# A two-layer bidirectional encoder trunk on one core: the convolution gate as 512-column products, and five small moves around it

## The chip, the cores and the metric

The kernel runs on one core of a Trainium2 chip. The metric is the time of one execution on the device in microseconds (us); lower is better. The engines are TensorE (PE; its weight loads are listed as PEld), VectorE (DVE), ScalarE (ACT), GpSimd (POOL) and SyncE (SP, which only issues DMAs here). Each engine works through its own list of instructions in order and waits on semaphores.

## The reference

Sequence 256, width 2048, two layers. Cut to what matters:

```python
h = x
for i in range(DEPTH):                       # DEPTH = 2
    hn = _rmsnorm(h, norm_g[i])
    u = hn @ w_in[i]
    a_val, a_glu, a_z, q, k, v, b_z = jnp.split(u, offs, axis=-1)
    ya = _conformer_conv(a_val, a_glu, ...)  # GLU, depthwise conv (31 taps), LayerNorm, SiLU
    ya = ya * jax.nn.silu(a_z)               # the convolution gate
    yb = _window_attention(q, k, v, bias_band, sink[i]) * jax.nn.silu(b_z)
    h = h + jnp.concatenate([ya, yb], axis=-1) @ w_out[i]
    e = _rmsnorm(p[i] @ w_pe[i], pe_g[i])
    h = h + e * jax.nn.sigmoid(h @ w_pg[i])  # the gate of the per-layer embedding
return _rmsnorm(h, final_g)
```

## The kernel before, in words

Everything is held with channels on the 128 partitions and the 256 positions along the free axis, so a tile of a product is 128 x 256. To keep float32 accuracy, activations and weights are split into a high part (rounded) and a low part (the rest): ACT casts the high part (L163 for weights), DVE subtracts (L166). A product is then high x high + high x low + low x high. mm3 has two forms. The narrow one adds three 256-column products into one half of a PSUM bank (L402 to L404). The wide one (wide, L399 and L400) streams both parts of the activations through the high weights at once, 512 columns, into the two halves of a bank, and adds the low weights' 256-column product to the second half; the two halves must then be added, which merge does with a copy on ACT (L410) and an add on DVE (L411).

Weights come in halves of 128 x 1024, eight k tiles of 128 columns each, in the order of weight_halves(), which is the order in which PE uses them. step takes one half and ends in a pump, which lets work written as generators go on: the convolution (conv, DVE), attention, the embedding's norm, and lnorm, the layer norm behind the convolution. get asks for the split of the weights four halves ahead.

A layer runs in this order: e (p times w_pe, L498), the RMS norm of h, the value and GLU products (ag), k, v, then four pairs of attention gate (zb) and q, then four pairs of the convolution gate (za, L707 for its SiLU). The second half of the last pair is preceded by finish, which lets convolution and attention end. Then yb, the attention's result, is split (L750 on ACT, L751 on DVE), the mean of the convolution is taken by PE (L716), and the output projection goes over the yb half of its weights for all 16 tiles and then over the ya half (wide form, L776 to L778 make h and its two parts, h1). Last comes the gate of the embedding (g, wide form) with w_pg.

An inverse root mean square needs a sum over partitions: rstd_col gets it by products with a column of ones (L349), raises it to -0.5 on POOL (L356), and DVE spreads it into a diagonal (L361); rstd_row multiplies that by ones (L367) to have it in every partition. rh is the norm of h, re that of e, rv that of the convolution, rf the final one.

At the start nothing is in flight: x comes in four loads, weights and p beside them, PE multiplies zeros (warm), and ACT squares x (L385, L388, L506) while it copies e's products out of PSUM (L522); DVE adds the squares (L389) and folds them (L376).

Of the kernel before, what the change touches and what calls it, by code (L numbers as in the profile page):

```python
# [54 lines left out]
AW = (0,0,0,0)  # L55
NWARM = 4
QQ = ((4, 5), (2, 4))
# [21 lines left out]
def weight_halves():  # L79
# [28 lines left out]
    for j in range(NB_FIRST, KT):  # L108
        out.append(("w_out", tile_cols(j), 8, 8))
        out.append(("w_out", tile_cols(j), 0, 8))  # L110
    for j in range(KT):
        std("w_pg", tile_cols(j))
# [13 lines left out]
def trunk_kernel(ctx: ExitStack, tc: tile.TileContext, xT, pT, wst, par, gain, relb, sinkp, onehot, out):  # L126
# [151 lines left out]
    load_half(0, 1)  # L278
    load_x(4, nc.scalar)
    load_x(0)  # L280
    load_half(1, 0, nc.scalar)
# [61 lines left out]

    def rstd_col(parts, dim, name, between=None, idles=0):

# [10 lines left out]
        nc.gpsimd.tensor_tensor(col, v, mhalf, ALU.pow)  # L356
        if between:
            between()
        dg = wk.tile([P, 2, P], F32, name=name + "dg", tag="rdg", bufs=1)
        for b in range(2):  # L360
            nc.vector.tensor_scalar(dg[:, b, :], ident, col[:, b:b + 1], None, ALU.mult)  # L361
        return dg

    def rstd_row(dg, name, tag="rb", copy=True):

        bb = bank(name + "b")
        nc.tensor.matmul(bb[:, 0, :], ones, dg.rearrange("p a b -> p (a b)"), start=True, stop=True)  # L367
        if not copy:
            return bb[:, 0, :]
        rb = wk.tile([P, S], F32, name=name + "rb", tag=tag, bufs=1)  # L370
        nc.scalar.copy(rb, bb[:, 0, :])
        return rb
# [22 lines left out]
    def mm3(o, w, x, start, stop):  # L395
# [8 lines left out]
        nc.tensor.matmul(o, w[:, 1], x[:, 0], start=False, stop=stop, skip_group_check=True)  # L404

    def merge(bs):

        t = wk.tile([P, 2, S], F32, name="hl", tag="ptt")[:, 0:len(bs), :]
        for x, b in enumerate(bs):
            nc.scalar.copy(t[:, x, :], b[:, 1, :])  # L410
            nc.vector.tensor_add(t[:, x, :], b[:, 0, :], t[:, x, :])  # L411
        return t
# [42 lines left out]
    for l in range(DEPTH):  # L455
# [21 lines left out]
        def operands(k, n):  # L477
            for k in range(k, k + 2 * n, 2):
                subs.append(operand(k))
                if len(subs) > 1:  # L480
                    subs.pop(0)()

        for q in range(4):
            n = Cursor.h
# [5 lines left out]
            for jj in range(0, 4, 2):  # L490
# [29 lines left out]
                if QQ[l][1] + (l == 0) <= j // 2 <= QQ[l][1] + 1:  # L520
                    operands(4 * (j // 2 - QQ[l][1]), 2)
                nc.scalar.copy(e[j // 8][:, j % 8:j % 8 + 2, :], b)  # L522
            pump()
# [174 lines left out]
        for t in range(0, NCT, 2):  # L698
            b = pair(hg, f"za{l}_{t}")
            if t == NCT - 2:  # L700
                finish(l)

                for k in (0, 4):
                    nc.gpsimd.dma_start(a[:, k:k + 4, :], hsrc[:, k:k + 4, :])
                yb = bigt(f"yb{l}", F32R)
                nc.scalar.copy(yb[:, 0, 0:2, :], zb[:, 0:2, :])
            nc.scalar.activation(za[:, t:t + 2, :], b, AF.Silu)  # L707

        ya = bigt(f"ya{l}", F32R)

        def lnorm(l=l, acc=acc, za=za, ya=ya, ysum=ysum, done=done):

            mb = bank("mean")
            parts = [ysum] + [acc[:, t, :] for t in done[-2:]]
            for x, a in enumerate(parts):
                nc.tensor.matmul(mb[:, 0, :], ones, a, start=(x == 0), stop=(x == len(parts) - 1))  # L716
            mu = wk.tile([P, S], F32, name="mu", tag="mu", bufs=1)
# [4 lines left out]
            for t in range(4):  # L722
                nc.vector.tensor_sub(q[t], q[t], bcast2(mu))
                square_acc(vacc, q[t], t == 0, nc.vector)
                if t % 2:
                    yield
            yield from wait(LY[0])
            dg = rstd_col(halves_of(vacc), W_CONV, f"rv{l}")
            yield from wait(LY[1])
# [94 lines left out]
        for j in range(0, KT - 2, 2):  # L824
            gate(j, merge([wide(h1, f"g{l}_{j + x}") for x in range(2)]))
            if j == 4 and not last:
                pp = wk.tile([P, 2, 2, S], F32R, name="pp", tag="qq")
                hilo(pp[:, 0], pp[:, 1], pf)
# [103 lines left out]
```

## Time and profile before

| | |
|---|---|
| runs of before | 980.79 us median of 3 (979.82 to 983.81) |
| the profiled execution's own time | 984.36 us |
| its span, first to last instruction | 982.6 us |
| mean granted clock of TensorE | 0.995 of full speed |
| busy: PE, DVE, ACT, POOL | 966.2, 796.8, 558.1, 82.2 us |

The profile is of one execution, so its rows add up to its own time, not to the median. A row of a timeline gives the start, the duration, the engine, the line of the kernel, the output and inputs, their shape and how many instructions were merged; in brackets stands how long the engine was idle before, and what ended that. Matmuls overlap, so their rate is read from start to start. A float32 product shows as two instructions.

### The profile page before, as it was taken

To read this page: it belongs to the slowest core of one execution; us is meant where nothing else is said; L and a number is where in the kernel's file an instruction comes from. 1 tells how busy PE (TensorE), PEld (TensorE's weight loads), DVE (VectorE), ACT (ScalarE), POOL (GpSimd) and SP (SyncE) were. 2 spreads that over 40 slices of the span, in tenths; PEclk is the share of its full clock that TensorE was granted. 3 is DMA by queue.
4 is the path that set the end of the run, shared out by engine and by line. 5 is a ranking of instruction groups with operands and counts; after the bars stand their busy time and mean duration, and the time that the engine had idled before them with its cause. 6 is when DMAs were issued, how large, how long until landed. Compare 5 with 4: busy or idle time off the path is not lost.

```text
span 982.6 us, 17720 instructions
## 1 busy us (share of the span) xinstructions
PE 966.2 (98%) x7196; PEld 913.1 (93%) x7196; DVE 796.8 (81%) x1383; ACT 558.1 (57%) x861; POOL 82.2 (8%) x79
## 2 busy tenths in 40 slices
PE   8999999999999999999999999999999999999995
PEld 6999999999999998888899999999999999888885
DVE  3899989987787777787689998988887877777763
ACT  4655454777774544555566444568778545445552
POOL 0022001010000000011103200000100000000111
PEclk9999999999999999999999999999999999999998
DMA  7674636555547454546546455465454555544532
GB/s 284 221 242 171 207 137 232 190 179 177 171 151 243 147 205 170 207 171 220 202 178 215 172 195 192 171 209 200 150 166 167 177 194 201 180 170 173 180 120 86
DMA packets 29005, 182.45 MB, mean 186 GB/s; under 512 B 3595, under 2 KB 4156, under 8 KB 9084
## 3 DMA queue, kind: packets, MB, share of 16 engines
q1 hardware_dynamic: 24284, 165.70, 48.3%
q0 software_dynamic: 3344, 12.88, 4.1%
q10 hardware_dynamic: 1296, 2.75, 0.8%
q8 instruction: 56, 0.92, 0.4%
q14 instruction: 25, 0.20, 0.1%
HBM read 177.09 MB, written 4.23 MB: 185 GB/s over the span
## 4 chain that ended last, share of the span: by engine, by line
PE 89%; DVE 5%; ACT 2%; issue 2%; DMA 1%; POOL 0%; SPq 0%; DVEq 0%; ACTq 0%; POOLq 0%
PE g L399 11%; PE ag L404 6%; PE ag L402 6%; PE ag L403 6%; PE g L400 5%; PE o L399 3%; PE za L402 3%; PE zb L402 3%; PE q L402 3%; PE o L402 3%; PE o L403 3%; PE o L404 3%; PE zb L403 3%; PE q L403 3%; PE za L403 3%; PE zb L404 3%
## 5 line engine op out<-in xcount | busy, mean ns | idle before, releaser
L166 DVE TENSOR_TENSOR w<-raw,w 128x1024 fp32r<-128x1024 f32 x306 | 372.8, 1227 | 102.9 <-ACT w L163 97.8
L163 ACT CAST w<-raw 128x1024 fp32r<-128x1024 f32 x308 | 314.5, 1046 | 167.3 <-PE ag L404 43.5
L572 DVE SCALAR_TENSOR_TENSOR cz<-az,pars,cz 128x241 f32<-128x241 f32 (+11 forms) x480 | 218.0, 504 | 1.0
L399 PE MATMUL g<-h,w 128*128 128x512 f32 x496 | 175.6, 399 | 2.3 <-DVE h L778 2.3
L404 PE MATMUL ag<-hg,w 128*128 128x256 f32 x512 | 145.1, 283 | 0.5 <-DVE w L166 0.5
L402 PE MATMUL ag<-hg,w 128*128 128x256 f32 x512 | 145.4, 284 | 0.0
L403 PE MATMUL ag<-hg,w 128*128 128x256 f32 x512 | 145.0, 283 | 0.0
L400 PE MATMUL g<-h,w 128*128 128x256 f32 x496 | 139.3, 281 | 0.0
L399 PEld LDWEIGHTS g<-h,w 128*128 128x128 f32 x496 | 93.2, 188 | 26.1 <-DVE h L778 2.9
L402 PEld LDWEIGHTS ag<-hg,w 128*128 128x128 f32 x512 | 98.3, 192 | 0.9 <-ACT cz L565 0.8
L404 PEld LDWEIGHTS ag<-hg,w 128*128 128x128 f32 x512 | 98.2, 192 | 0.8 <-DVE w L166 0.7
L403 PEld LDWEIGHTS ag<-hg,w 128*128 128x128 f32 x512 | 98.3, 192 | 0.1
L400 PEld LDWEIGHTS g<-h,w 128*128 128x128 f32 x496 | 93.7, 189 | 0.0
L399 PE MATMUL o<-ya,w 128*128 128x512 f32 x256 | 90.5, 399 | 0.0
L402 PE MATMUL za<-hg,w 128*128 128x256 f32 x256 | 73.7, 288 | 0.0
L402 PE MATMUL o<-yb,w 128*128 128x256 f32 x256 | 73.3, 286 | 0.0
L402 PE MATMUL q<-hg,w 128*128 128x256 f32 x256 | 73.3, 286 | 0.0
L402 PE MATMUL zb<-hg,w 128*128 128x256 f32 x256 | 73.1, 286 | 0.0
L403 PE MATMUL o<-yb,w 128*128 128x256 f32 x256 | 72.6, 283 | 0.0
L404 PE MATMUL o<-yb,w 128*128 128x256 f32 x256 | 72.4, 283 | 0.0
L403 PE MATMUL zb<-hg,w 128*128 128x256 f32 x256 | 72.4, 283 | 0.0
L403 PE MATMUL q<-hg,w 128*128 128x256 f32 x256 | 72.4, 283 | 0.0
(231 smaller groups left out, 2093.7 us busy)
## 6 DMA issues: line engine op xcount, KB each, us to landing
raw<-in_wst SPq DMA_DIRECT2D x153, 1024.0 KB, 4.9
bias<-fscr POOLq DMA_DIRECT2D x16, 384.0 KB, 3.8
raw<-in_wst SPq DMA_DIRECT2D x4, 512.0 KB, 7.9
az<-in_xT POOLq DMA_DIRECT2D x4, 512.0 KB, 6.1
hscr<-e POOLq DMA_DIRECT2D x2, 1024.0 KB, 5.0
az<-hscr POOLq DMA_DIRECT2D x4, 512.0 KB, 6.2
x<-in_xT SPq DMA_DIRECT2D x3, 512.0 KB, 8.1
out_t<-og ACTq DMA_DIRECT2D x4, 256.0 KB, 3.2
```

Of the source, the lines that this page charges most:

```text
L163: nc.scalar.copy(hi, raw)
L166: nc.vector.tensor_sub(lo, raw, hi.bitcast(F32))
L399: nc.tensor.matmul(o, w[:, 0], x, start=start, stop=False, skip_group_check=True)
L400: nc.tensor.matmul(o[:, 1], w[:, 1], x[:, 0], start=False, stop=stop, skip_group_check=True)
L402: nc.tensor.matmul(o, w[:, 0], x[:, 0], start=start, stop=False, skip_group_check=True)
L403: nc.tensor.matmul(o, w[:, 0], x[:, 1], start=False, stop=False, skip_group_check=True)
L404: nc.tensor.matmul(o, w[:, 1], x[:, 0], start=False, stop=stop, skip_group_check=True)
L572: nc.vector.scalar_tensor_tensor(acc[:, t, lo_:hi_], a[:, t, lo_ + s:hi_ + s], w(k), acc[:, t, lo_:hi_], ALU.mult, ALU.add)
```

## The change

- The convolution gate uses the wide form, one bank for each of the 16 tiles. A pair is merged (L408 and L409 in the new file) before its SiLU, for the last pair behind finish and the first cast of yb.
- lnorm adds the last two convolution tiles to the running sum on DVE and yields once; PE takes the mean from that one tile, one step later. The sums of squares are folded before the column sum.
- rstd_col returns the column itself. rstd_row multiplies a broadcast of the column with the identity, 128 columns for each half; the diagonals are gone.
- The first two tiles of the embedding's gate are interleaved, both over the first half of h1 and then both over the second, with the weights in that order.
- In layer 0 the copies of e's first four products come after all squares of x; x tiles 0 to 3 are loaded from ACT's queue and 4 to 7 from SP's; six warm products instead of four.

```diff
-NWARM = 4
+NWARM = 6
...
-    for j in range(KT):
+    for k0 in (0, 8):
+        for j in range(2):
+            out.append(("w_pg", tile_cols(j), k0, 8))
+    for j in range(2, KT):
         std("w_pg", tile_cols(j))
...
     load_half(0, 1)
-    load_x(4, nc.scalar)
-    load_x(0)
+    load_x(0, nc.scalar)
+    load_x(4)
...
         nc.gpsimd.tensor_tensor(col, v, mhalf, ALU.pow)
-        if between:
-            between()
-        dg = wk.tile([P, 2, P], F32, name=name + "dg", tag="rdg", bufs=1)
+        return col
+
+    def rstd_row(col, name, tag="rb", copy=True):
+
+        bb = bank(name + "b")
         for b in range(2):
-            nc.vector.tensor_scalar(dg[:, b, :], ident, col[:, b:b + 1], None, ALU.mult)
-        return dg
-
-    def rstd_row(dg, name, tag="rb", copy=True):
-
-        bb = bank(name + "b")
-        nc.tensor.matmul(bb[:, 0, :], ones, dg.rearrange("p a b -> p (a b)"), start=True, stop=True)
+            nc.tensor.matmul(bb[:, 0, b * P:(b + 1) * P], col[:, b:b + 1].broadcast_to([P, P]), ident,
+                             start=b == 0, stop=b == 1, skip_group_check=True)
...
+    def merge1(t, b):
+
+        nc.scalar.copy(t, b[:, 1, :])
+        nc.vector.tensor_add(t, b[:, 0, :], t)
...
-                nc.scalar.copy(e[j // 8][:, j % 8:j % 8 + 2, :], b)
+                ecopy.append((j, b))
+
+                while ecopy and (l or j // 2 >= 3):
+                    jc, bc = ecopy.pop(0)
+                    nc.scalar.copy(e[jc // 8][:, jc % 8:jc % 8 + 2, :], bc)
...
         for t in range(0, NCT, 2):
-            b = pair(hg, f"za{l}_{t}")
+            bs = [wide(hg, f"za{l}_{t + x}") for x in range(2)]
             if t == NCT - 2:
                 finish(l)
...
                 nc.scalar.copy(yb[:, 0, 0:2, :], zb[:, 0:2, :])
-            nc.scalar.activation(za[:, t:t + 2, :], b, AF.Silu)
+            for x in range(2):
+                merge1(za[:, t + x, :], bs[x])
+            nc.scalar.activation(za[:, t:t + 2, :], za[:, t:t + 2, :], AF.Silu)
...
+            for t in done[-2:]:
+                nc.vector.tensor_add(ysum, ysum, acc[:, t, :])
+            yield
             mb = bank("mean")
-            parts = [ysum] + [acc[:, t, :] for t in done[-2:]]
-            for x, a in enumerate(parts):
-                nc.tensor.matmul(mb[:, 0, :], ones, a, start=(x == 0), stop=(x == len(parts) - 1))
+            nc.tensor.matmul(mb[:, 0, :], ones, ysum, start=True, stop=True)
...
+            vs = fold(vacc)
             yield from wait(LY[0])
-            dg = rstd_col(halves_of(vacc), W_CONV, f"rv{l}")
+            dg = rstd_col([vs], W_CONV, f"rv{l}")
...
-            gate(j, merge([wide(h1, f"g{l}_{j + x}") for x in range(2)]))
+            if j:
+                bs = [wide(h1, f"g{l}_{j + x}") for x in range(2)]
+            else:
+                bs = [bank(f"g{l}_{x}") for x in range(2)]
+                for n in range(2):
+                    for b in bs:
+                        step(b, h1, n == 0, n == 1)
+            gate(j, merge(bs))
```

What this does to the engines' order is shown at three places. First DVE in layer 0, from the last split of weights under the convolution gate to the first work of the normalisation. Before (w are split weights, yb the attention's result, cz the convolution and its gate):

```order
L166 TENSOR_TENSOR w_3504<-raw_3354,w_3504 128x1024 [waits DMAHW5_49,Activation_49]
L572 SCALAR_TENSOR_TENSOR cz_258<-az_257,pars,cz_258 128x241 [waits DVE_49]
L166 TENSOR_TENSOR w_3532<-raw_3354,w_3532 128x1024 [waits Activation_49]
L751 TENSOR_TENSOR yb_3561<-az_257,yb_3561 128x512 [waits Activation_49] x4
L166 TENSOR_TENSOR w_3583<-raw_3433,w_3583 128x1024 [waits DMAHW6_49,PE_49,Activation_49]
L723 TENSOR_TENSOR cz_258<-cz_258,mu 128x512
```

DVE at the same place in the changed kernel:

```order
L169 TENSOR_TENSOR w_3406<-raw_3283,w_3406 128x1024 [waits DMAHW5_49,Activation_49]
L581 SCALAR_TENSOR_TENSOR cz_258<-az_257,pars,cz_258 128x241 [waits DVE_49]
L169 TENSOR_TENSOR w_3426<-raw_3283,w_3426 128x1024 [waits Activation_49]
L409 TENSOR_TENSOR cz_258<-za_6_3349,cz_258 128x256 [waits Activation_49]
L409 TENSOR_TENSOR cz_258<-za_7_3403,cz_258 128x256 [waits Activation_49]
L764 TENSOR_TENSOR yb_3447<-az_257,yb_3447 128x512
L764 TENSOR_TENSOR yb_3447<-az_257,yb_3447 128x512 [waits Activation_49] x3
L725 TENSOR_TENSOR ysum_259<-ysum_259,cz_258 128x256 [waits Pool_49]
L725 TENSOR_TENSOR ysum_259<-ysum_259,cz_258 128x256 [waits DVE_49]
L169 TENSOR_TENSOR w_3469<-raw_3350,w_3469 128x1024 [waits DMAHW6_49,PE_49,Activation_49]
```

Two adds of the merge, each waiting for ACT's copy, now stand ahead of yb's four subtractions, and two adds of the channel sums behind them.

PE between the last gate product and the output projection of layer 0, before (o is a tile of the projection):

```order
L403 MATMUL za_6_3432<-hg_1_310,w_3397 128x256
L404 MATMUL za_6_3432<-hg_1_310,w_3397 128x256
L716 MATMUL mean<-ysum_259,ones 128x256 [waits PE_49,Pool_49]
L716 MATMUL mean<-cz_258,ones 128x256 [waits DVE_49] x2
L402 MATMUL o_0_3580<-yb_3561,w_3435 128x256 [waits PE_49,Activation_49]
L403 MATMUL o_0_3580<-yb_3561,w_3435 128x256 [waits DVE_49]
L404 MATMUL o_0_3580<-yb_3561,w_3435 128x256
```

PE there in the changed kernel, with the rest of the first weight half left out:

```order
L399 MATMUL za_7_3403<-hg_1_310,w_3318 128x512
L400 MATMUL za_7_3403<-hg_1_310,w_3318 128x256
L402 MATMUL o_0_3466<-yb_3447,w_3352 128x256 [waits PE_49,Activation_49]
L403 MATMUL o_0_3466<-yb_3447,w_3352 128x256 [waits DVE_49]
...
L404 MATMUL o_0_3466<-yb_3447,w_3352 128x256
L728 MATMUL mean<-ysum_259,ones 128x256 [waits DVE_49,PE_49]
L402 MATMUL o_0_3466<-yb_3447,w_3379 128x256
```

The projection follows the gate directly; the mean, one matmul instead of three, stands behind the projection's first weight half.

ACT at the start of the program, before (hacc and sq are squares of x, e the products of p, raw and w the weights):

```order
L385 ACTIVATE hacc<-x 128x512
L388 ACTIVATE sq<-x 128x512
L522 COPY e_129<-e 128x512
L388 ACTIVATE sq<-x 128x512 x2
L522 COPY e_129<-e 128x512
L388 ACTIVATE sq<-x 128x512 x2
L522 COPY e_129<-e 128x512
L388 ACTIVATE sq<-x 128x512
L506 ACTIVATE sq<-x 128x512
L522 COPY e_129<-e 128x512
L163 CAST w_201<-raw_98 128x1024
```

ACT there in the changed kernel:

```order
L385 ACTIVATE hacc<-x 128x512
L388 ACTIVATE sq<-x 128x512 x6
L511 ACTIVATE sq<-x 128x512
L531 COPY e_131<-e 128x512 x4
L166 CAST w_200<-raw_100 128x1024
```

All eight squares now come ahead of the four copies of e.

## Rows read from the trace of the kernel before

**Rows 1.** The page: busy us (share of the span) and instructions of each engine.
```profile
PE 966.2 (98%) x7196; PEld 913.1 (93%) x7196; DVE 796.8 (81%) x1383; ACT 558.1 (57%) x861; POOL 82.2 (8%) x79
```
**Rows 2.** Waits of PE: us in total, times, longest us.
```profile
PE g L399 <- DVE h L778: 2.3, 2, 1.1
PE e L498 <- DMA raw<-in_wst: 1.5, 2, 1.2
...
PE rh0c L349 <- DVE fold L376: 1.0, 1, 1.0
PE rfb L367 <- DVE rfdg L361: 0.6, 1, 0.6
```
**Rows 3.** DMA issues of the first 40 us: KB each, median us to landing.
```profile
x<-in_xT ACTq DMA_DIRECT2D x1, 512.0 KB, 9.0
```
**Rows 4.** Timeline of the start.
```profile
1.67 0.45 ACTq L272 DMA_DIRECT2D x<-in_xT  x1
...
8.10 7.17 PE L498 MATMUL e<-p,raw 128*128 128x256 f32 x32 [0.30 <-DMA raw<-in_wst]
...
9.69 0.63 ACT L385 ACTIVATE hacc<-x 128x512 f32<-128x512 f32 x1 [5.71 <-DMA x<-in_xT]
...
10.87 0.69 DVE L389 TENSOR_TENSOR hacc<-hacc,sq 128x512 f32<-128x512 f32 x1 [9.47 <-ACT sq L388]
...
11.87 3.88 DVE L389 TENSOR_TENSOR hacc<-hacc,sq 128x512 f32<-128x512 f32 x5 [0.31 <-ACT sq L388]
...
15.78 0.42 DVE L376 TENSOR_TENSOR fold<-hacc 128x256 f32<-128x256 f32 x1
...
17.62 3.58 PE L498 MATMUL e<-p,raw 128*128 128x256 f32 x8
```
**Rows 5.** Stretch 18 to 20 us: us, busy of each engine, PEclk, DMA share, GB/s.
```profile
18.00:20.00 2.00, 2.00 (x6) 1.61 (x5) 1.22 (x3) 1.05 (x2) 0.70 (x1) 0.50 1.01 374
```
**Rows 6.** PE timeline: convolution gate (13 steps apart), then embedding's gate (104 steps apart).
```profile
277.06 0.28 PE L402 MATMUL za<-hg,w 128*128 128x256 f32 x1
...
281.74 0.28 PE L402 MATMUL za<-hg,w 128*128 128x256 f32 x1
...
406.49 0.40 PE L399 MATMUL g<-h,w 128*128 128x512 f32 x1
...
443.24 0.40 PE L399 MATMUL g<-h,w 128*128 128x512 f32 x1
```
**Rows 7.** Timeline of one merge in the embedding's gate, layer 1.
```profile
956.95 0.37 ACT L410 COPY hl<-g 128x256 f32<-128x256 f32 x1 [1.45 <-PE g L400]
...
957.36 0.42 DVE L411 TENSOR_TENSOR hl<-g,hl 128x256 f32<-128x256 f32 x1 [0.54 <-ACT hl L410]
```
**Rows 8.** DVE timeline behind the second pair of the convolution gate, layer 0.
```profile
284.06 1.22 DVE L166 TENSOR_TENSOR w<-raw,w 128x1024 fp32r<-128x1024 f32 x1 [3.69 <-ACT w L163]
```
**Rows 9.** PE timeline, gate to projection, layer 0: last gate product, first and second half's first.
```profile
305.39 0.28 PE L404 MATMUL za<-hg,w 128*128 128x256 f32 x1
...
306.62 0.47 PE L402 MATMUL o<-yb,w 128*128 128x256 f32 x1
...
309.73 0.28 PE L402 MATMUL o<-yb,w 128*128 128x256 f32 x1
```
**Rows 10.** ACT and DVE timelines at the same place.
```profile
305.71 0.60 ACT L707 ACTIVATE cz<-za 128x512 f32<-128x512 f32 x1 [1.31 <-PE za L404]
306.20 1.65 ACT L750 CAST yb<-az 128x512 fp32r<-128x512 f32 x3
...
306.85 1.90 DVE L751 TENSOR_TENSOR yb<-az,yb 128x512 fp32r<-128x512 f32 x3 [1.11 <-ACT yb L750]
```
**Rows 11.** DVE timeline: the last low part of ya, layer 0.
```profile
347.01 0.69 DVE L744 TENSOR_TENSOR ya<-cz,ya 128x512 fp32r<-128x512 f32 x1
```
**Rows 12.** Chain that ended last: start us, us, what.
```profile
125.30 0.34 PE re0c L349 x4
...
321.41 0.79 PE rv0c L349 x8
```

More of the change, by code (lines that the diff above doesn't have):

```diff
@@ L342, in idle, with rstd_col @@
             nc.tensor.matmul(wb[:, 0, 0:P], ones, ident, start=True, stop=True)
-    def rstd_col(parts, dim, name, between=None, idles=0):
+    def rstd_col(parts, dim, name, idles=0):
         c = bank(name + "c")
@@ L409, in merge @@
         for x, b in enumerate(bs):
-            nc.scalar.copy(t[:, x, :], b[:, 1, :])
-            nc.vector.tensor_add(t[:, x, :], b[:, 0, :], t[:, x, :])
+            merge1(t[:, x, :], b)
         return t
@@ L481, in operands @@
                     subs.pop(0)()
+        ecopy = []
         for q in range(4):
```

## The prediction, on record before the changed kernel ran

> **What bounds the kernel now.** I read the busy shares first. TensorE (PE) is busy for 966.2 of the 982.6 us span, while VectorE (DVE) has 796.8 and ScalarE (ACT) 558.1 [rows 1]. So only two things can move the time: how long the matmul stream itself takes, and the places where it waits. The list of PE's waits came next [rows 2]. All of them together are under 10 us. The largest are 2.3 us at the start of the gate of the per-layer embedding (1.1 us in each layer, for the last low part of h1 from L778), 1.5 us for the first weights and 0.6 us in the tail. PE also waits 1.0 us for the folded squares of x near the start. No saving in a helper engine counts unless it shortens one of these, and every new wait of PE counts in full.
>
> **The change part by part.** The profiled execution took 984.36 us (span 982.6 and 1.8 us around it); the runs' median is 980.79. I sum changes against 984.36 and carry the sum over to the median.
>
> *Start.* The first x tiles (0 to 3) go from SP's queue to ACT's, where they stand behind two weight loads, and tiles 4 to 7 take their old place. In the trace the x load in ACT's queue was issued at 1.67 and took 9.0 us, so it landed at 10.7 [rows 3, 4]. The first square started at 9.69, when SP's load had landed [rows 4]. With the places swapped, I expect the first square about 1.0 us later, at 10.7, and the first add of squares at 11.9 instead of 10.87. The copies of e leave the squares' way, so that adds no longer wait for squares. But the adds depend on each other: five took 3.88 us and the fold began 0.8 us after the last one started, so from 11.9 the fold comes after six adds at about 0.8 us each, at 16.6 instead of 15.78 [rows 4]. Loss: 0.8 us. If the landing does not depend on the place in the queue, the fold starts at 15.6, a gain of 0.2. I take 0.8, because both loads were issued within 0.01 us and the only difference between them was the queue.
> Behind the fold the trace shows eight matmul instructions of e in 3.58 us, at a granted clock of 0.50, where 32 of the same form took 7.17 us before [rows 4, 5]. At the full clock eight take 1.8 us, so the low stretch costs 1.8 us. It followed the wait for the fold and the one-column products of the column sums. The wait is not shorter in my sum, so I leave this cost where it is. The bound on the other side is that the clock holds: 1.8 us gained.
> The two more warm-up products (four instructions) fall in the 1.2 us in which PE waited for the first weights [rows 2]; at 0.22 us each they need 0.9 us there, and 0.6 us more than the cover if they ran at half speed. I take 0. The DVE work on diagonals (0.5 us each) leaves, but at rh, re and rv PE did not wait for it; that counts only in the tail.
>
> *Convolution gate.* Each k step was three 256-column products: 13 steps from 277.06 to 281.74, 0.360 us each. A step with a 512-column product and a 256-column one took 36.75/104 = 0.3534 us [rows 6]. The durations of single rows (283 against 399 ns) would promise far more, but they overlap; start to start is what counts. 16 weight halves of 8 steps in 2 layers are 256 steps at 0.0066: 1.7 us gained.
> The Trainium skill, "TensorE: Matmul & The Clock Gate", section "Back-to-back issue gap", gives a warm product N/2.4 ns plus about 2.5 ns; joining two products would then save one 2.5 ns, 0.6 us in all, and the sum below would lose 1.1 us of its gain. The trace's 120 ns for 256 columns disagrees with that rule (109 ns).
> The merges cost ACT two copies of 0.37 and DVE two adds of 0.42 per pair of tiles [rows 7]. Behind the first three pairs they are covered: DVE stood idle 3.69 us behind one such pair [rows 8], and get() asks for the split of the weights four halves before their use. I take 0. Without that cover each pair would cost its 0.8 us of adds, six pairs 5 us.
>
> *Start of the output projection.* This is the place that speaks against the change. In the order of DVE the adds of the last two gate tiles now stand ahead of the four subtractions that make yb's low part, and ACT's casts of yb stand behind the silu of the merged tiles. PE's second product of the projection needs that low part. The mean's products, which stood ahead of the projection and gave 1.1 us of cover, now come behind its first weight half.
> Let E be the end of the last gate product: 305.39 + 0.28 = 305.67 [rows 9]. ACT starts 0.04 later [rows 10]; a copy takes 0.37 and DVE's add follows 0.41 after its start, 0.42 long [rows 7]. So the last add runs to E+0.9, the first subtraction, 0.6 to 0.7 long, ends at E+1.5, and PE, which arrives at E-0.16, waits 1.6 us. ACT's silu waits for the add and starts at E+1.0; the casts follow 0.5 us later and 0.5 us apart (306.20 behind 305.71, three in 1.65), to E+2.1, 2.6 and 3.1 [rows 10]. Subtractions end at E+2.8, 3.4 and 4.0. PE goes at 0.12 us a product, reaches tile 2 at E+2.2 and waits until E+2.8, then runs through, and ends its first half at E+4.9. One mean matmul (two of the six instructions that filled the 1.1 us between the last gate product's slot and 306.62) adds 0.37: the second half starts at E+5.2. Before it started at 309.73, E+4.1 [rows 9]. That is 1.15 us lost per layer, 2.3 in both, with the shorter mean already in it. Bounds: if the low part is ready in time, the second half starts at E-0.16+2.88+0.37 = E+3.1, a gain of 1.9 in both; if the clock falls in that wait, 3.6 more is lost (below).
> Later in this stage the normalisation runs one pump later, plus one fold on DVE. Its last result landed at 347.7 [rows 11]; the halves that read it come behind 16 halves on yb and could not start before 309.73 + 15 x 2.88 = 352.9. A delay of 3 to 4 us is hidden there.
>
> *Column sums.* rv's two column products instead of four: eight instructions took 0.79, four of the same form 0.34 [rows 12]. 0.45 per layer, 0.9 gained. Broadcasting by two 128-column products in place of one with 256 streams the same columns: 0.
>
> *Gate of the embedding.* With tiles 0 and 1 interleaved, 16 instructions (2.8 us) of tile 1's first half stand between PE and the half that needs the late part of h1. The wait was 1.1 us. All of it goes: 2.3 gained [rows 2]. Nothing else is late there; the other weights were split before.
>
> *Tail.* PE waited 0.6 us for the diagonals [rows 2]. Now it waits for the power itself, which becomes the stationary operand and cannot be loaded ahead; I take 0.4 of the 0.6 as gained, with 0 and 0.6 as bounds.
>
> Sum: +0.8 - 1.7 + 2.3 - 0.9 - 2.3 - 0.4 = -2.2 us. 984.36 becomes 982.2, the median **978.6**.
>
> **The rivals.**
> *The wait at the projection does not come* (the merge's adds get through ahead, or the yb parts are ready). For it: ACT and DVE were nearly idle at E. Against it: the order of DVE's queue. Sum -2.2 - 2.3 - 1.9 = -6.4: 974.4.
> *The clock holds at the start.* For it: the squares are no longer interrupted, and a longer run of warm products. Against it: my count makes the wait before the column sums longer. It gains 1.8, and up to 1.0 with the wait itself and the 0.8 that I count as lost: 975 to 976.
> *The clock falls at the projection's start* (slower). PE would stand 1.6 us, work 0.7, and stand 0.6. In the trace a wait of 1.0 us and the one-column products behind it were followed by clock 0.50 [rows 5], whereas 1.1 us of wait at the embedding's gate, with full products on both sides, was followed by steps at the full rate [rows 2, 6]. A stretch like that costs 1.8. One keeps the change ahead by 0.4; with both layers it turns, 982.2, slower than before. Beyond 985.7 it would have to last twice as long in both layers.
> The Trainium skill, same page, section "HAM oscillation — how this bites in real kernels", says that idle gaps of PE bring the low clock back until steady work lifts it; that is this rival's rule, and the rows show both outcomes.
> *The change does not do what it says* in one place: squares of x are first in ACT's order, but their data come later. That is in the sum.
>
> **How the numbers follow.** Forecast 0.60 (977 to 981); no wait at the projection 0.13; clock holds at the start 0.12; clock falls at the projection 0.12; something larger, such as weights split too late behind the merges, 0.03. A measurement of this kernel tells about 0.5% from no change, so 975.9 and 985.7 are the bounds. Faster: most of the second case and half of the third, 0.18. Slower: 0.04, from the last two. Same: 0.78. The range 973.5 to 983.5 holds the forecast, most of the second and third case and the fourth; what is outside is all gains together (near 971) and a longer low clock.
>
> **What would show it.** Narrow steps of 0.360 us replaced by 0.353 in the convolution gate; a new wait of PE on DVE's yb of 1.5 us and one of 0.6 in each layer; the 1.1 us waits on L778 gone, and rfb's 0.6 replaced by a shorter one on GpSimd; the first square near 10.7, the fold near 16.6, and e's eight instructions still at 0.43 us. The prediction is wrong if the projection starts without a wait, if the granted clock in it falls below 1, or if gate products wait for split weights.

## The result and the profile after

The changed kernel takes 984.15 us (median of 22 executions, 982.72 to 985.79), the kernel before 981.33 us (22 executions beside them); the ratio is 1.0023, with an interval of 1.0014 to 1.0031. By the ratio it is slower by 2.3 us (1.4 to 3.0), by the medians by 2.8. A gain of 2.2 us was predicted, from a median of 980.79 over three executions. Two executions that ran far slower, one of the kernel before (5342 us) and one of e15 (1336 us), are left out of the comparisons.

The busy shares of the changed kernel's profiled execution (983.59 us, span 981.1):

```profile
PE 964.6 (98%) x6944; PEld 899.9 (92%) x6944; DVE 800.1 (82%) x1391; ACT 562.7 (57%) x877; POOL 82.6 (8%) x79
```

PE's waits, which answer to [rows 2]:

```profile
PE o L403 <- DVE yb L764: 4.2, 4, 1.8
PE rh0c L352 <- DVE fold L376: 1.7, 1, 1.7
PE warm L259 <- DVE zeros L256: 1.2, 1, 1.2
PE rfc L352 <- ACT sq L820: 0.4, 1, 0.4
```

The two waits of 1.1 us on h1 are gone. In their place PE waits 4.2 us for yb's low part, twice in each layer, and 1.7 instead of 1.0 us for the fold at the start. The timeline of DVE and ACT behind the last gate product of layer 0 (304.19 in the second list):

```profile
304.95 0.75 DVE L409 TENSOR_TENSOR cz<-za,cz 128x256 f32<-128x256 f32 x2
305.61 0.68 DVE L764 TENSOR_TENSOR yb<-az,yb 128x512 fp32r<-128x512 f32 x1
306.90 1.90 DVE L764 TENSOR_TENSOR yb<-az,yb 128x512 fp32r<-128x512 f32 x3 [0.61 <-ACT yb L763]
...
305.73 0.63 ACT L718 ACTIVATE cz<-cz 128x512 f32<-128x512 f32 x1 [0.86 <-DVE cz L409]
306.27 1.64 ACT L763 CAST yb<-az 128x512 fp32r<-128x512 f32 x3
```

and PE at the same place, with the first product of the convolution gate and the first on ya in both layers:

```profile
249.95 0.40 PE L399 MATMUL za<-hg,w 128*128 128x512 f32 x1
...
304.19 0.28 PE L400 MATMUL za<-hg,w 128*128 128x256 f32 x1
304.30 0.28 PE L402 MATMUL o<-yb,w 128*128 128x256 f32 x1
306.35 0.38 PE L403 MATMUL o<-yb,w 128*128 128x256 f32 x1 [1.77 <-DVE yb L764]
...
307.65 0.38 PE L403 MATMUL o<-yb,w 128*128 128x256 f32 x1 [0.32 <-DVE yb L764]
...
310.06 0.47 PE L402 MATMUL o<-yb,w 128*128 128x256 f32 x1
310.37 0.28 PE L403 MATMUL o<-yb,w 128*128 128x256 f32 x1
...
354.31 0.40 PE L399 MATMUL o<-ya,w 128*128 128x512 f32 x1
...
725.58 0.40 PE L399 MATMUL za<-hg,w 128*128 128x512 f32 x1
...
831.43 0.40 PE L399 MATMUL o<-ya,w 128*128 128x512 f32 x1
```

This is the chain that was predicted: two adds of the merge, then the subtraction, then PE. With E, the end of the last gate product, at 304.47, the first subtraction ends at E+1.8 and the projection's second half starts at E+5.6; E+1.5 and E+5.2 were predicted. What the forecast had only as a rival stands in the windows of layer 0 (304 to 312) and layer 1 (780 to 788); columns: window, its length, busy time of PE, PEld, DVE, ACT and POOL with instructions, granted clock, DMA share, GB/s:

```profile
304.00:308.00 4.00, 1.91 (x13) 1.46 (x13) 3.39 (x6) 2.64 (x6) 0.66 (x2) 1.00 0.60 195
308.00:312.00 4.00, 4.00 (x34) 3.95 (x33) 2.90 (x6) 2.18 (x3) 0.95 (x2) 1.00 1.01 399
...
780.00:784.00 4.00, 1.91 (x14) 1.50 (x14) 3.39 (x7) 3.02 (x6) 1.05 (x2) 1.00 0.59 155
784.00:788.00 4.00, 4.00 (x22) 3.82 (x21) 2.32 (x4) 0.98 (x3) 0.59 (x2) 0.57 1.00 398
```

The waits are the same in both layers, but in layer 1 the granted clock fell to its lower level behind them, and PE issued 22 products where layer 0 had 34. From the first product of the convolution gate to the first on ya ("the stage" below), layer 0 takes 104.36 us and layer 1 105.85 (before: 104.05 in each). A stretch at the lower clock, a low stretch for short, costs 1.5 us.

At the start, ACT's and DVE's first rows on x, e behind the column sums, and a window behind that:

```profile
10.43 0.63 ACT L385 ACTIVATE hacc<-x 128x512 f32<-128x512 f32 x1 [6.42 <-DMA x<-in_xT]
...
16.33 0.42 DVE L376 TENSOR_TENSOR fold<-hacc 128x256 f32<-128x256 f32 x1
...
18.17 2.46 PE L503 MATMUL e<-p,raw 128*128 128x256 f32 x8
...
20.00:22.00 2.00, 2.00 (x8) 1.82 (x7) 0.79 (x3) 0.48 (x1) 0.00 (x0) 0.50 0.19 70
```

The fold is 0.55 us later than before [rows 4]. The clock falls here too, but only behind most of these eight instructions, which take 2.46 us for 3.58. Last, the run's time less its span is 1.7 to 1.9 us in the executions of the kernel before, and 2.4 to 2.5 in all but one (2.9) of the changed kernel's 22.

### The profile page after: what moved, and what is told of

Same layout as the page of the kernel before. It is cut to its first block, busy times and chain, and to the rows that moved or that the text cites. A ratio compares the mean times of both kernels' runs of the same rounds, so it can differ in the third digit from the quotient of the medians.

```text
span 981.1 us, 17233 instructions
## 1 busy us (share of the span) xinstructions
PE 964.6 (98%) x6944; PEld 899.9 (92%) x6944; DVE 800.1 (82%) x1391; ACT 562.7 (57%) x877; POOL 82.6 (8%) x79
## 4 chain that ended last, share of the span: by engine, by line
PE 95%; DVE 3%; DMA 1%; issue 0%; ACT 0%; ACTq 0%; DVEq 0%
PE g L399 12%; PE ag L402 6%; PE ag L404 6%; PE ag L403 6%; PE o L399 6%; PE g L400 6%; PE za L399 5%; PE zb L402 3%; PE q L402 3%; PE o L403 3%; PE zb L403 3%; PE q L403 3%; PE zb L404 3%; PE q L404 3%; PE o L404 3%; PE o L402 3%
## 5 line engine op out<-in xcount | busy, mean ns | idle before, releaser
L399 PE MATMUL za<-hg,w 128*128 128x512 f32 x256 | 92.2, 402 | 0.0
```

The source lines that it names most:

```text
L399: nc.tensor.matmul(o, w[:, 0], x, start=start, stop=False, skip_group_check=True)
```

## The experiments

Two theories at first. **W**: only the length of the new waits counts. **C**: the waits at the projection's start also bring the low clock. A third, **M**, came up on the way. All ratios are to the kernel before, run beside the variant; each is known to some 0.1% or 1 us (0.17% for e16), so a difference of two to about 1.3 us. Where that is too coarse, only a trace can decide.

### The start of the projection

**e1: the last pair's merge behind yb.** The changed kernel, with the last pair's merge and SiLU behind yb's subtractions:

```diff
-            for x in range(2):
-                merge1(za[:, t + x, :], bs[x])
-            nc.scalar.activation(za[:, t:t + 2, :], za[:, t:t + 2, :], AF.Silu)
+            if t < NCT - 2:
+                for x in range(2):
+                    merge1(za[:, t + x, :], bs[x])
+                nc.scalar.activation(za[:, t:t + 2, :], za[:, t:t + 2, :], AF.Silu)
...
+        for x in range(2):
+            merge1(za[:, NCT - 2 + x, :], bs[x])
+        nc.scalar.activation(za[:, NCT - 2:NCT, :], za[:, NCT - 2:NCT, :], AF.Silu)
         lgen = lnorm()
```

> The changed kernel (984.2 us), but the merges and the SiLU of the convolution gate's last pair stand behind the casts and subtractions of yb, so that PE's second product of the projection is ready sooner. Theory W (the wait alone costs): PE's waits on yb of 1.8 and 0.3 us in each layer go, 4.2 us in both: 980.0. Theory C (the wait invites stretches of granted clock 0.5, some 1.7 us each): the same 4.2, and on top one to two stretches of the projection's start gone: 976.6 to 978.3, with a mean granted clock that rises from 0.993-0.995 to 0.996 or more. Third theory (the late normalisation costs): no gain or a loss, since this edit makes it later still.

981.11 us, ratio 0.9991 (0.9981 to 1.0). The trace has one wait of 1.1 us for yb in each layer, one of 0.3 for the mean, and no low clock in the projection. Neither theory's number came, since both had the waits gone. By the ratios 3.1 us below the changed kernel. The waits shrank from 4.2 to 2.9 us, and the stage by 0.7 us in layer 0 (103.65 for 104.36), where no low stretch had been, but by 2.2 in layer 1 (103.67 for 105.85), where one was. So the waits don't make up the gain.

**e2: cover without a shorter chain.** The changed kernel, with products on a constant (a tile of ones and the identity, not zeros) while PE would stand:

```diff
         h1 = []
+        idle(8)
         for j in range(0, KT, 2):
```

> The changed kernel with 16 instructions of products on zeros (about 1.75 us at the full rate) put ahead of the output projection in each layer; the projection still can't go on before yb's low part is there. Theory C: PE never stands there, so the granted clock stays at 1 and the time falls by the stretches avoided, one to two of 1.7 us: 980.8 to 982.5. Theory W: the products only fill the wait: 984.2, within 0.5.

981.53 us, ratio 1.0001 (0.9992 to 1.0011), 2.2 us below the changed kernel by the ratios. Its stage takes 104.36 and 104.35 us, to 0.01 what the changed kernel's takes without a low stretch: nothing is done sooner. But the windows show

```profile
304.00:308.00 4.00, 3.67 (x28) 3.24 (x27) 3.39 (x7) 2.51 (x6) 0.55 (x1) 1.00 0.63 209
...
784.00:788.00 4.00, 4.00 (x34) 3.95 (x33) 2.90 (x5) 1.93 (x3) 0.71 (x2) 1.00 1.00 403
```

a clock of 1.00 in both layers. In the stage nothing but the clock differs; W alone falls.

**e5 and e6: the two causes apart.** The kernel before with one part each: in e5 all pairs wide and merged as in the change, the mean ahead of the projection; in e6 only the mean's edit. The diffs are e5's and e6's:

```diff
+    def merge1(t, b):
+
+        nc.scalar.copy(t, b[:, 1, :])
+        nc.vector.tensor_add(t, b[:, 0, :], t)
...
-            b = pair(hg, f"za{l}_{t}")
+            bs = [wide(hg, f"za{l}_{t + x}") for x in range(2)]
...
-            nc.scalar.activation(za[:, t:t + 2, :], b, AF.Silu)
+            for x in range(2):
+                merge1(za[:, t + x, :], bs[x])
+            nc.scalar.activation(za[:, t:t + 2, :], za[:, t:t + 2, :], AF.Silu)
```

```diff
+            for t in done[-2:]:
+                nc.vector.tensor_add(ysum, ysum, acc[:, t, :])
+            yield
             mb = bank("mean")
-            parts = [ysum] + [acc[:, t, :] for t in done[-2:]]
-            for x, a in enumerate(parts):
-                nc.tensor.matmul(mb[:, 0, :], ones, a, start=(x == 0), stop=(x == len(parts) - 1))
+            nc.tensor.matmul(mb[:, 0, :], ones, ysum, start=True, stop=True)
```

> The kernel before (981.4 us) with only the convolution gate in the wide form and the merges where the change puts them; the mean's three products stay ahead of the projection, where they keep PE at work for 1.1 us. Both theories: the gate's steps gain 0.85 us in each layer, and PE's second product waits for yb's low part some 0.5 us instead of 1.8. Theory W: the projection's second half starts 0.8 us later behind the gate's end, so the sum is about nil: 981.4, within 0.7. Theory C: the waits that are left are short and come behind work, so the granted clock falls in the projection seldom: the same 981.4; if it falls as often as in the changed kernel, 983 or more, and the length of the wait is not what calls it.

> The kernel before with only the mean's change: channel sums folded on DVE, one mean matmul in place of three, behind the projection's first weight half; the gate stays narrow and unmerged. PE loses its cover and waits about 1.1 us for yb's low part in each layer. Theory W: what PE waits it had spent on the mean before, so the second half starts at the same time: 981.4, within 0.7. Theory C: a wait of that length without a merge brings the low clock in many executions: 982.5 to 984.5, and stretches of 3.4 us at 0.5 in the projection in the trace.

e5: 981.73 us, ratio 0.9996 (0.9984 to 1.0008), waits of at most 0.5 us. e6: 981.74 us, ratio 0.9993 (0.998 to 1.0005). e6 did not make the wait that it was meant to make (PE stood 0.2 and 0.3 us, not 1.1: without merges yb is ready at once), so its expectation for C was not tested. No low clock in the projection of either, and no loss.

**e13: the two together**, both diffs on the kernel before.

> The kernel before (981.6 us) with only two of the change's parts: the convolution gate wide with all its merges, and the mean behind the projection's first half. Apart neither moved the time. Theory C: together they make PE wait 1.8 and 0.3 us at yb in each layer as in the changed kernel; 0.7 us a layer for the wait (rv still has four column products) and the low stretch in two of three projections: 985 to 985.7. Theory W: the waits alone, 983.0. If they don't act together: 981.6. Time outside the span: 2.5 us if these two make it, else 1.8.

985.29 us, ratio 1.0035 (1.0021 to 1.0049): 3.4 us lost by two parts that cost nothing singly. PE in layer 0:

```profile
304.48 0.28 PE L402 MATMUL o<-yb,w 128*128 128x256 f32 x1
306.53 0.39 PE L403 MATMUL o<-yb,w 128*128 128x256 f32 x1 [1.77 <-DVE yb L759]
...
307.84 0.58 PE L403 MATMUL o<-yb,w 128*128 128x256 f32 x1 [0.33 <-DVE yb L759]
308.22 0.42 PE L404 MATMUL o<-yb,w 128*128 128x256 f32 x1
308.43 0.41 PE L402 MATMUL o<-yb,w 128*128 128x256 f32 x1
308.64 0.41 PE L403 MATMUL o<-yb,w 128*128 128x256 f32 x1
```

The starts are 0.21 us apart instead of 0.12 from the second wait on, in both layers; the stage takes 106.23 and 106.28 us, 2.2 more than before, of which 1.5 is the clock.

**e10 and e14: take out one of the two.** The changed kernel, in e10 with the last pair narrow and unmerged, in e14 with the mean's three products ahead of the projection again (e6's diff the other way round). e10's edit:

```diff
-            bs = [wide(hg, f"za{l}_{t + x}") for x in range(2)]
             if t == NCT - 2:
+                b = pair(hg, f"za{l}_{t}")
                 finish(l)
+            else:
+                bs = [wide(hg, f"za{l}_{t + x}") for x in range(2)]
+                for x in range(2):
+                    merge1(za[:, t + x, :], bs[x])
+                b = za[:, t:t + 2, :]
+            if t == NCT - 2:
...
-            for x in range(2):
-                merge1(za[:, t + x, :], bs[x])
-            nc.scalar.activation(za[:, t:t + 2, :], za[:, t:t + 2, :], AF.Silu)
+            nc.scalar.activation(za[:, t:t + 2, :], b, AF.Silu)
```

> The changed kernel (984.2 us) with the last pair of the convolution gate narrow and without a merge. Theory W: yb's low part is ready 0.9 us sooner, PE's wait of 1.8 us falls to about 0.3 to 0.9 in each layer; 2 to 2.9 us gained, 0.2 lost to the narrow steps: 981.5 to 982.5. Theory C: the waits that are left are too short for the low clock, the stretches of the projection go too: 979.8 to 981. The time outside the span: 2.5 us if it doesn't hang on this merge, 1.8 if it does.

> The changed kernel (984.2 us) with the mean's three products back ahead of the projection as a cover, and all merges kept. Theory C: the wait of 1.8 us falls to some 0.5, 0.4 us a layer are gained, and the low stretches of the projection go: 980.5 to 981.5. Theory W: 0.4 us a layer: 983.4. Time outside the span: 1.8 us if it needs the late mean.

e10: 978.91 us, ratio 0.9974 (0.9964 to 0.9985), a wait of 0.9 us in each layer; that is below what either theory had (979.8 at the least). e14: 981.19 us, ratio 0.9998 (0.9984 to 1.0011), in each layer waits of 0.5 and 0.3 us for yb and a new one of 0.5 for rv's column; C had 980.5 to 981.5, W 983.4. Neither has low clock in the projection. With the last pair of the four in each layer left as it was, the change is a gain of 2.5 us.

### The gate of the embedding

**e4: the interleave alone**, on the kernel before.

```diff
-    for j in range(KT):
+    for k0 in (0, 8):
+        for j in range(2):
+            out.append(("w_pg", tile_cols(j), k0, 8))
+    for j in range(2, KT):
...
-            gate(j, merge([wide(h1, f"g{l}_{j + x}") for x in range(2)]))
+            if j:
+                bs = [wide(h1, f"g{l}_{j + x}") for x in range(2)]
+            else:
+                bs = [bank(f"g{l}_{x}") for x in range(2)]
+                for n in range(2):
+                    for b in bs:
+                        step(b, h1, n == 0, n == 1)
+            gate(j, merge(bs))
```

> The kernel before (981.3 us) with only the first two tiles of the embedding's gate interleaved. If the wait of 1.1 us in each layer was all there was to it: 979.0 (2.3 less). If the wait comes back behind the interleaved half, or is given back at the next barrier: 981.3. Between: 980.2, one layer only.

980.44 us, ratio 0.9983 (0.9973 to 0.9993): 1.7 us (0.7 to 2.7) of the 2.3. From this gate's first product to e of layer 1 it takes 90.45 us, 1.37 less than before's profiled execution (91.82). But e5 and e6, with the 1.1 us wait, take 90.21 there. The same steps run faster in them, which led to theory M.

**e9: the kernel before again**, unchanged.

> The kernel before once more, unchanged, for a second trace of it. Theory M (new, beside C): behind the 1.1 us wait in the gate of the embedding the wide steps go on at one of two rates, 2.826 or 2.773 us a weight half, drawn anew in each layer and each execution; the profiled execution had the slow one in both layers. Then this trace shows 91.8 or 90.2 us between the start of that gate and e of layer 1, 97.4 or 95.9 us between its start in layer 1 and the last product, each with half the chance, and its span follows them. If the rate belongs to the kernel: 91.8 and 97.4 again.

979.72 us, with the 1.1 us wait in both layers, and 90.22 and 95.89 us where the first trace had 91.82 and 97.41. The start of this stage and of e behind it, and four steps some 16 us behind the wait:

```profile
397.96 0.40 PE L399 MATMUL g<-h,w 128*128 128x512 f32 x1
...
419.89 0.40 PE L399 MATMUL g<-h,w 128*128 128x512 f32 x1
420.12 0.28 PE L400 MATMUL g<-h,w 128*128 128x256 f32 x1
420.24 0.39 PE L399 MATMUL g<-h,w 128*128 128x512 f32 x1
420.47 0.27 PE L400 MATMUL g<-h,w 128*128 128x256 f32 x1
420.58 0.40 PE L399 MATMUL g<-h,w 128*128 128x512 f32 x1
...
420.93 0.39 PE L399 MATMUL g<-h,w 128*128 128x512 f32 x1
...
421.28 0.40 PE L399 MATMUL g<-h,w 128*128 128x512 f32 x1
...
488.19 0.28 PE L402 MATMUL e<-pp,w 128*128 128x256 f32 x1
```

1.39 us for four steps, 0.347 each, where [rows 6] gave 0.3534, at a granted clock of 1.00 in both. The 13 steps ahead of the wait still take 0.353 in this trace. M holds: code and clock are the same and the period is another. In the seven traces with the wait (before, e5, e6, e7, e9, e13, e16) the 14 gates had the short period 9 times and the long one 5 times; in the eleven interleaved ones, 22 gates, it was always the long one.

**e16: the changed kernel without the interleave.**

> The changed kernel with the embedding's gate not interleaved. Theory M: the wait of 1.1 us comes back in each layer and behind it either rate: 0.2 us less or 1.4 more in a layer than interleaved, so 983.8, 985.4 or 987 for one execution, 985.3 in the mean. If the wait alone counted: 986.4. Time outside the span: 1.8 us if it needs the interleaved gate, else 2.5.

986.56 us, ratio 1.0028 (1.0011 to 1.0045), 983.40 to 988.05 over 8 executions. The trace has the long period in layer 0 (91.81 us) and the short one in layer 1. The median is nearer the second expectation, the spread fits the first. By the ratios it is 0.5 us above the changed kernel, by the medians, which were not taken side by side, 2.4; the size is left open. A third figure comes from the traces: over the 14 gates with the wait the long period costs 1.4 us more than interleaved and the short one 0.2 less, which makes the interleave worth 0.7 us an execution.

### The start and the norms

**e3, e7, e11: the start.** e3 is the changed kernel with the two x loads in their old places, e11 with the whole start as before, e7 the kernel before with the new start.

```diff
-    load_x(0, nc.scalar)
-    load_x(4)
+    load_x(4, nc.scalar)
+    load_x(0)
```

> The changed kernel with the x loads in the places that they had before (tiles 4 to 7 on ACT's queue, 0 to 3 on SP's). Theory W: the first square starts at 9.4 to 9.7 in place of 10.43 and the fold by as much earlier: 0.7 to 1.0 us less, 983.3. Theory C: PE's wait for the fold falls from 1.7 to 0.9 us, and the low stretch of the clock at the start with it in most executions: up to 2.6 less, 981.6. If the landing doesn't depend on the place in the queue: 984.2.

> The kernel before with only the edits of the start: x tiles 0 to 3 on ACT's queue, all squares ahead of the copies of e, six warm products. Theory W: the fold comes 0.5 to 0.8 us later: 982.0. Theory C: PE's wait ahead of the column sums grows from 1.0-1.3 to 1.7 us and nearly every execution has the low stretch behind it, which the kernel before has in a part of them: 982.5 to 983, with a mean granted clock of 0.995 where most runs of before have 0.996 to 0.998. If the time outside the span also comes from here, it rises from 1.75 to 2.5 us.

> The changed kernel with the whole start as before: x loads, copies of e between the squares, four warm products. From the parts: 0.4 us for the later e at the start, 0.5 for the wait, and the low stretch at the start in fewer executions: 982.5 to 983.3, with the projection's stretches as in the changed kernel. If the start's edits cost nothing: 984.2. The time outside the span: 1.8 us if it comes from the start together with another part, else 2.5.

e3: 983.15 us, ratio 1.001 (0.9999 to 1.002). e7: 982.06 us, ratio 1.0002 (0.9991 to 1.0014). e11: 983.53 us, ratio 1.0017 (1.0008 to 1.0025). The start's edits cost between 0 and 1.3 us, and the intervals don't part these. The traces give a narrower figure: with the new start the convolution gate of layer 0 begins 0.3 to 0.4 us later in the mean (249.95 to 250.77 us in five traces with a low stretch at the start, for 249.87 to 250.19 in four with the old start; 249.08 to 249.29 in three without one, for 248.57 to 249.04 in four; e3 and e12, with parts of either, not counted). The low stretch behind the start's column sums shows no dependence on these edits: it is in 5 of 8 traces with them and in 4 of 9 without (e3, with a part of them, not counted). It goes with the wait: 9 of 14 traces in which PE waits 0.8 us or more for the fold have it, none of the 4 in which it doesn't (e5, e6, e9, e12).

**e15: the diagonals and rv's four column products back** in the changed kernel.

> The changed kernel with the diagonals, their broadcast and rv's four column products back. Both theories: 0.45 us a layer for the column products and 0.5 in the tail lost: 985.5, with the clock as in the changed kernel. Time outside the span: 1.8 us if it needs the broadcast columns, else 2.5.

985.27 us (one execution), low clock in both projections. Its tail, from the last gate's first product on, is 96.02 us against 95.47: 0.55 gained by the change there, 0.4 predicted. From the projection's second half to the ya half it takes 44.68 us in each layer against 44.25: rv's four column products cost 0.43 more than two, where 0.45 was predicted.

### A version that beats both

**e8** takes the kernel before with the wide gate for the first three pairs of the four in each layer, the interleave, the broadcast columns and rv's fold, and leaves start and mean alone. **e12** adds

```diff
-LY = (2, 1)
+LY = (2, 2)
...
-                        hparts = [fold(hacc)] + halves_of(sq)
+                        hparts = halves_of(sq) + [fold(hacc)]
...
+                    if l == 0:
+                        idle(4)
                     dg = rstd_col(hparts, D, f"rh{l}")
```

> A version meant to beat both: the start, the mean and the projection's start as before; the convolution gate wide for its first seven pairs and narrow, without a merge, for the last; the embedding's gate interleaved; the broadcast of the column in place of diagonals, and rv's squares folded. Both theories, from the kernel before at 981.4: 1.3 to 2.8 for the embedding's gate, 1.5 for the wide steps, 0.9 for rv, 0.5 in the tail: 975.7 to 977.2, with no wait of PE on yb and a granted clock of 1 at the projection. If the extra 0.7 us outside the span comes with the broadcast or the wide gate, 976.4 to 977.9.

> The combined version (980.0 us) with the one-column products of the last squares ahead of those of the fold and eight short products on zero use ahead of them (PE stood 1.4 us there), and the broadcast of rv one step later, since PE now waited 0.5 us for it in each layer. Theory W: 0.4 to 0.7 us at the start and 1.0 at rv gained: 978.4. Theory C: the stretch of low clock at the start, which eight of ten executions of the combined version seem to have, goes as well: 977.0, with a mean granted clock of 0.997.

e8: 980.04 us, ratio 0.9973 (0.9964 to 0.9982), less than expected: its trace shows a new wait of 0.5 us in each layer for rv's column, a low stretch at the start, and the long period in both gates. e12: 976.27 us, ratio 0.995 (0.9937 to 0.9962). Its waits of PE, all that are left:

```profile
PE warm L259 <- DVE zeros L256: 1.2, 1, 1.2
PE e L503 <- DMA raw<-in_wst: 0.7, 2, 0.4
PE ag L404 <- DVE w L169: 0.5, 1, 0.5
PE rfc L352 <- ACT sq L821: 0.4, 1, 0.4
```

By the ratio that is 4.9 us less than before. Of the 3.8 us by which its span is below e8's (974.5 for 978.3; by the ratios it is 2.3), its trace has 2.4 at the start (from e's first product to that of ag 17.05 us for 19.42), where the wait was 1.4 and the rest is the clock, as C expects, and 0.75 a layer at rv.

## Why the prediction was wrong

**The step that failed** is the clock at the projection's start. The sum put it at nothing and left it to a rival: "The clock falls at the projection's start" got 0.12, because waits of 1.1 us at the embedding's gate had been followed by full rate. The mechanism, the place and the cost were as the rival put them (1.5 us a stretch, 1.8 predicted). But it was the rule: in the six traces with the 1.8 us wait (the changed kernel, e3, e11, e13, e15, e16) 10 of 12 projections start with a low stretch; in the twelve traces whose longest wait there is 1.1 us or less, none of 24 does. That is 10/12 x 2 x 1.5 = 2.5 us an execution, and e2 measured 2.2. The forecast went by the wait of 1.1 us as the nearer row, and the wait that it had itself worked out was longer. The rival's own time, 982.2, is 1.4 us above its base where 2.3 to 2.8 was measured; the rest lies in the terms below.

The Trainium skill, "TensorE: Matmul & The Clock Gate", section "HAM oscillation — how this bites in real kernels", shows idle gaps between blocks of products bringing the low clock back, each at its cost. The traces agree on the mechanism; in its example the gaps are longer than the blocks of products between them, and here one gap of 1.8 us with one of 0.3 behind it, amid hundreds of us of products, was enough in 10 of 12.

**The sum's base was an untypical execution.** The 2.3 us for the embedding's gate were worked out from a trace with the long period behind both waits. The two periods make 1.6 and 1.5 us in the two layers (91.82 and 97.41 against e9's 90.22 and 95.89), and before's executions have either. Over both, the interleave is worth 1.7 us by e4's ratio and 0.7 by the count of periods, not 2.3. Moving a sum from the profiled execution (984.36) to the median (980.79) took for granted that each term was in the median too; e9 shows another execution of the same code, 4.6 us shorter. The median itself, of three executions, was 0.5 us below that of 22.

**The projection's start**, clock aside, was sized too low by 0.4 us a layer: E+5.6 for the second half against E+5.2, since the merge's two adds ended 0.3 us later than counted. The convolution gate itself gained 0.98 us a layer (54.23 for 55.21), where 0.85 was predicted, since some 30 of its 128 steps took 0.347 us; the second half's start to the ya half is 0.25 us shorter, where 0.45 was counted for rv. rv did save its 0.43 (e15); 0.18 went to the first product behind the mean, which takes 0.31 us to the next instead of 0.12 (310.06 to 310.37) and which the late mean moves into this part (e6, with the late mean alone: 44.67 for 44.50).

**Right**: the new waits' place and order (1.8 and 0.3 us; 1.6 and 0.6 predicted), the merges hidden behind the first pairs, the waits on L778 gone, the fold at 16.33 (16.6), the delayed normalisation hidden, the tail. **Wrong in a small way**: the warm products were not free; e starts at 6.18 instead of 5.80 us, and 0.6 us later in the mean of the nine traces with six of them than in the nine with four. The sign that e's eight instructions would still take 0.43 us each did not come, since the clock fell later (0.31 in the mean). And the rival with the clock held at the start, given as 975 to 976, is 976.8 by its own terms if the clock alone is gained.

**0.7 us outside the span** were in no step. It rises only where the last pair is merged and the mean is late: 2.1 us in e13 and e15, 2.45 in the changed kernel, e1, e2, e3, e11 and e16, and 1.8 in e5, e6, e10 and e14, which lack one of the two. What lies there no trace shows; its cause stays open.

Together, for the median: 2.2 to 2.5 for the clock, 0.6 for the stages from the gate to the ya half (0.31 each, clock aside), 0.7 outside the span, 0.3 to 0.4 at the start, less 0.7 to 1.7 at the embedding's gate and 0.55 in the tail: 1.6 to 3.0, and 2.3 to 2.8 was measured.

## What to carry to other kernels

A wait that is moved costs more than its length if it grows: PE's waits between full products brought no low clock up to 1.1 us, and at 1.8, with one of 0.3 behind it, they did in 10 of 12 cases, at some 1.5 us each. Nothing between was tried, nor the long wait without the short one. Where a chain can't be shortened, products that compute nothing are a cover; better is to leave the last tile, whose result the next stage's start stands behind, in the form that needs no merge. And one trace is one execution: before a sum is made on it, a second trace of the same kernel shows which terms are there every time.

## What the hardware showed unexpectedly

- The same stream of 512- and 256-column products at the same granted clock of 1.00 has two periods, 0.353 and 0.347 us a step. Which one it is, is settled at a break in the stream and then holds, for the 80 us of the stage at the embedding's gate; behind the wait there it differs from layer to layer and from execution to execution. A wait is not needed: in the wide convolution gate the steps behind the first two of three groups of transposes (pt, eight 128-column products) take the short period, and those behind the third the long one, in both layers of every trace that has it. What settles it was not tried.
- Parts that cost nothing singly (0.9996 and 0.9993) cost 0.35% together.
- The time outside the span changed with edits in the middle of the program, by 0.3 to 0.7 us.
